# Attention steps of one unit laid between the projection chunks of the next, with their matmuls in a fixed order

## The chip, the cores and the metric
One NeuronCore of one Trainium2 chip runs the whole kernel. The metric is the device time of one execution in microseconds (us). TensorE is called PE in the rows (its weight loads PEld), VectorE DVE, ScalarE ACT, GpSimd POOL, SyncE SP.

## What is computed
One decoder layer over a prompt of 1024 tokens and, at once, one new token for each of 8 sequences with caches (T = 1032 columns). The part that the change touches is the first norm and the grouped, dilated attention of the prompt:

```
h = rms_norm(x) ; proj = h @ w_in            # f32, 1024 inputs
for g in 0..2:                               # windows 128, 512, 2048; dilations 1, 4, 16
    s = q_g k_g^T * Dh^-0.5 + bias_g         # 8 heads of 64, blocks of 128 queries,
    s = where(band mask, s, -inf)            #   keys of the own and the previous block
    o_g, lse_g = softmax(s) @ v_g, logsumexp(s)
a_out = sum_g softmax_g(lse_g) * o_g         # the groups are combined
```

Beside it stand the sample tokens' attention over the caches, the mLSTM with its gates, the gated merge, and a ConvFFN. All arithmetic has f32 inputs and outputs.

## The kernel before
**Projections.** f32 products are made of three products of high and low parts. A weight tile of 1024 x 128 arrives as `raw`; `split` (L175) casts it to `whi` on ScalarE (L176) and subtracts to get `wlo` on VectorE (L177). `mm` (L182) issues 24 matmuls into one PSUM bank (L189): 8 of whi with the activation's high part, 8 of whi with its low part, 8 of wlo with its high part. `proj_chunk` does that for one of three column chunks (352, 352, 328) and writes the bank out; `proj` does the three. There are 3 such banks (`pp`), 5 banks (`X`) for everything else, two buffers for whi and wlo and three for raw. A pool of 16 tiles of 128 x 1032 (`A`) holds what lives longer.

**The first norm.** Nine row tiles are loaded by SP, normalised in an order that is written out (every ScalarE and VectorE step of it is pinned by `in_order`), transposed on TensorE and split into `act_hi`, `act_lo` (L241, L247). The raw weights of the first q and k are loaded between them and split after tiles 1 and 2.

**Attention.** There are 12 units: pair of heads p = 0 to 3, and in it group g = 0 to 2; unit number 3p + g. A unit makes the projections q, k, v (nine chunks, written out to `qT`, `kT` by ScalarE, L338 and L340, to `vT` by VectorE, L342), transposes v and k back to rows (`ptr`, L365; copies `vn`, `kn`), sends these to the caches by POOL, loads two bias tiles `bt`, and then runs its attention in slots. In slot x stand: the scores of group x (`stage_s`: matmuls L429, on VectorE a reduction with bias and minimum into `sb` and `st`, L438, on ScalarE the exponential, L442), the product of group x-2 (`stage_v`: `po` L482, written out to `oT` by L494 or L498), and the transposes of group x-1 (`stage_t`: `pt` L455, copied to `pts` by either engine, L458). Groups 0 and 1 have 4 groups of two blocks and so 6 slots, group 2 has 2 groups of four blocks and 4 slots.

**Between the units** stand the combining of the pair before and the sample tokens' attention: `combine_a` and `sample_a` at the end of a pair; then `combine_b` and `sample_b` after unit (p,0) of the next, `combine_c` and `sample_c` after unit (p,1), `sample_d` after unit (p,2). `combine_c` issues three loads `fbc` on POOL, each 1024 factors of a head read 64 times from `f_d`, multiplies each `oT` by its `fbc` on VectorE (L555), and adds (L556, L557). `sample_b` loads the broadcast q rows `qb` by POOL and multiplies by cache keys (L577). The mLSTM gates' projection (`gates_proj`, evacuated to `gsb`) comes after unit 0, four gate projections (`gate_a`) after unit 11.

**The order.** Each engine runs its instructions in one fixed order, which the framework chooses when the kernel is built: each instruction goes out by its place in the program as soon as it is ready by the framework's own durations, so that work of two units may mix. `in_order` binds an instruction to stay behind the one written before it on its engine. In a stage, every matmul but the first is bound so (`chained`, L411 on).

Of the kernel before, what the change touches and what calls it, by code (L numbers as in the profile page):

```python
# [22 lines left out]
DIL = (1, 4, 16)  # L23
# [17 lines left out]
def kernel(  # L41
# [48 lines left out]
    def A(name, cols=T, dt=F32):  # L90
        return ap_.tile([128, cols], dt, tag="A", name=name)
# [15 lines left out]
    def dma_out(out, in_):  # L107
        nc.gpsimd.dma_start(out=out, in_=in_)  # L108
# [49 lines left out]
    def raw_w(src):  # L158

        k = src.shape[0] // 128  # L160
        m = src.shape[1]
        raw = wp.tile([128, 1024], F32, tag="raw", name="wraw", bufs=3)
        dma_w(raw[:, 0:k * m].rearrange("p (k c) -> p k c", c=m), src.rearrange("(k p) c -> p k c", p=128))
        return raw, k, m

    def split_w(raw, k, m, pin=False):

        hi = wp.tile([128, 1024], F32R, tag="hi", name="whi")
        lo = wp.tile([128, 1024], F32R, tag="lo", name="wlo")
        return split(raw, hi, lo, k * m, pin) + (m,)  # L170

    def load_w(src):
        return split_w(*raw_w(src))
# [147 lines left out]
    def perm(ap, g):  # L321
        return ap.rearrange("p (r u) -> p u r", r=DIL[g]) if g else ap

    def attn_unit(pair, g, st):
        d = DIL[g]
        U = S // d
        qT, kT, vT = A("qT"), A("kT"), A("vT")
        evacs = []
        for kind, dst in enumerate((qT, kT, vT)):
            def evac(ci, t0, n, ps, kind=kind, dst=dst):  # L330
                npm = min(n, S - t0)
                if g == 0:
                    dv, sv = dst[:, t0:t0 + npm], ps[:, 0:npm]
                else:
                    dv = dst[:, 0:S].rearrange("p (r u) -> p r u", r=d)[:, :, t0 // d:(t0 + npm) // d]
                    sv = ps[:, 0:npm].rearrange("p (u r) -> p r u", r=d)
                if kind == 0:
                    nc.scalar.mul(dv, sv, -0.125)  # L338
                elif kind == 1:
                    nc.scalar.copy(dv, sv)  # L340
                else:
                    nc.vector.tensor_copy(dv, sv)  # L342
                if npm < n:
                    if kind == 0:
                        nc.vector.tensor_scalar(out=smp[:, pair, kind, g, :], in0=ps[:, npm:n], scalar1=-0.125, scalar2=None, op0=ALU.mult)
                    else:
                        nc.vector.tensor_copy(smp[:, pair, kind, g, :], ps[:, npm:n])
            col = kind * AQ + g * 512 + pair * 128
            if pair == 0 and g == 0 and kind < 2:
                evacs.append(evac)  # L350
                if kind == 1:
                    for ci in range(len(CHUNKS)):
                        for k in range(2):
                            proj_chunk(first_w[k], hT, evacs[k], ci)
            else:
                proj(w_in2[:, col:col + 128], hT, evac)
        vn = A("vn")
        kn = A("kn")
        keep = ((7,), (1, 3, 5, 7), tuple(range(8)))[g]
# [27 lines left out]
        for hd in range(2):  # L387
# [10 lines left out]
        oT = A("oT")  # L398
        live = {}
        pos = [None, None]  # L400

# [99 lines left out]
        for x in range(n + 2):  # L501
# [271 lines left out]
    def gate(dst, col):  # L773
# [2 lines left out]

        proj(w_in2[:, col:col + 128], hT, evac)

    def gate_a(j):
# [37 lines left out]
    def row_tile():  # L817
        return wk.tile([128, 128], F32, tag="rowsT", name="rowsT", bufs=4)

    done = None  # L820
    for pair in range(4):
        st = wk.tile([128, 96], F32, tag="st", name="st", bufs=2)
        oT = []
        for g in range(3):
            oT.append(attn_unit(pair, g, st))
            if g == 0 and done:
                combine_b(done[0])
                sc = sample_b(done[0])
            if g == 1 and done:
                combine_c(*done)  # L830
                sb = sample_c(done[0], sc)
            if g == 2 and done:
                sample_d(done[0], *sb)
            stage = pair * 3 + g
            if stage == 0:
                gates_proj()
            elif stage == 1:
                gates_log()
            elif stage == 2:
                gates_max()  # L840
            elif stage == 3:
                gates_rows()
            elif stage == 5:
                gcol, decb, sc8, scb3 = gates_cols()
            elif stage == 7:
                mcv_r = rows_load([mconv_w[0].rearrange("i (j p) -> (i j) p", p=128), mconv_b.rearrange("o (j p) -> (o j) p", p=128)], row_tile)
                mst_r = rows_load([st_conv[0].rearrange("b i (j p) -> (b i j) p", p=128)], row_tile)
            elif stage == 8:
                mcv = rows_T(mcv_r, c2.tile([128, 80], F32, name="mcv"))
                mcv3 = mcv.rearrange("p (i j) -> p i j", j=16)  # L850
                nc.vector.tensor_scalar(out=mcv3[:, :, 0:8], in0=mcv3[:, :, 0:8], scalar1=0.5, scalar2=None, op0=ALU.mult)
                nc.vector.tensor_scalar(out=mcv3[:, :, 8:16], in0=mcv3[:, :, 8:16], scalar1=1.0 / 32.0, scalar2=None, op0=ALU.mult)
                mst = rows_T(mst_r, c2.tile([128, 384], F32, name="mst"))
                mst4 = mst.rearrange("p (b i j) -> p j b i", b=8, i=3)
        combine_a(pair, st)
        sample_a(pair)
        done = (pair, oT)
# [8 lines left out]
    combine_c(*done)  # L866
    for g in range(3):
        for kv in range(2):
            for pair in range(4):
# [616 lines left out]
```

## Time and profile before

| what | us |
|---|---|
| median of 3 runs | 2315.59 |
| lowest and highest of them | 2315.16, 2315.99 |
| the profiled execution | 2312.85 |
| its span | 2311.0 |
| TensorE busy in the span | 2264.6 |
| VectorE, ScalarE, POOL busy | 1152.1, 686.6, 211.4 |

The span runs from the first to the last instruction of the profiled execution; 1.85 us of its time lie around it. Rows are of that execution. The attention phase lies between about 42 and 700 us; what follows (mLSTM, merge, ConvFFN) is not touched. A group of rows gives the number of instructions in it; a bracket gives the idle time of the engine just before it and what ended it.

### The profile page before, as it was taken

What the parts mean: (1) busy time and instruction counts of PE and PEld (TensorE: products, weight loads), DVE (VectorE), ACT (ScalarE), POOL (GpSimd) and SP (SyncE); (2) the same over time, 40 slices, a digit from 0 to 9 for tenths busy, and PEclk for the clock granted to TensorE, in tenths of its full rate; (3) what the DMA queues carried; (4) which work ended last, traced back from release to release, by engine and by line L of the source; (5) the groups of instructions that cost most, each with busy time, mean ns of one, the idle gap of its engine ahead of it and who ended that gap; (6) DMA issues with size and microseconds to landing.
All of it is one profiled execution on the core that took longest, in us unless ns stands there. A gap on an engine that the chain in (4) does not pass through costs nothing.

```text
span 2311.0 us, 36395 instructions
## 1 busy us (share of the span) xinstructions
PE 2264.6 (98%) x15077; PEld 2174.5 (94%) x15077; DVE 1152.1 (50%) x2689; ACT 686.6 (30%) x1337; POOL 211.4 (9%) x380
## 2 busy tenths in 40 slices
PE   7999999999999999999999999999999999999998
PEld 6799899989989999999999999999999999999997
DVE  6253434434435454646331444346556556655666
ACT  4234333343312333323232311342222222221222
POOL 1111210111110011111122100000000000000000
PEclk9999999999999999999999999999999999999999
DMA  5323533434362142424244521221111111111112
GB/s 186 93 52 83 121 79 97 115 82 120 95 187 82 51 127 59 128 60 137 77 128 130 200 72 46 74 78 59 55 37 46 37 46 55 55 48 43 48 37 78
DMA packets 243014, 196.79 MB, mean 85 GB/s; under 512 B 24393, under 2 KB 220089, under 8 KB 242834
## 3 DMA queue, kind: packets, MB, share of 16 engines
q1 hardware_dynamic: 206577, 124.65, 19.2%
q0 software_dynamic: 36272, 69.84, 9.9%
q8 instruction: 118, 1.93, 0.4%
q14 instruction: 47, 0.38, 0.1%
HBM read 160.30 MB, written 39.20 MB: 86 GB/s over the span
## 4 chain that ended last, share of the span: by engine, by line
PE 84%; DMA 5%; issue 3%; ACT 2%; DVE 1%; POOL 1%; DVEq 0%; POOLq 0%; ACTq 0%
PE pp L189 64%; PE ppd L1379 10%; DMA fbc<-f_d 3%; PE pcm L996 1%; ACT sb L442 1%; PE ni L990 1%; PE po L482 1%; PE pt L455 1%; PE s L429 1%; PE na L993 1%; PE sm L977 1%; PE pxo L1247 1%; PE ptr L365 0%; POOL out_dram L108 0%; PE pkm L966 0%
## 5 line engine op out<-in xcount | busy, mean ns | idle before, releaser
L189 PE MATMUL pp<-act_hi,whi 128*128 128x352 f32 (+1 forms) x3272 | 598.5, 324 | 4.4 <-ACT qT L338 2.0
L189 PE MATMUL pp<-act_lo,whi 128*128 128x352 f32 (+1 forms) x3272 | 585.2, 320 | 0.0
L189 PE MATMUL pp<-act_hi,wlo 128*128 128x352 f32 (+1 forms) x3272 | 581.1, 319 | 1.1 <-DVE wlo L177 1.1
L189 PEld LDWEIGHTS pp<-act_hi,whi 128*128 128x128 f32 x3272 | 527.5, 188 | 14.2 <-issue 4.3
L189 PEld LDWEIGHTS pp<-act_hi,wlo 128*128 128x128 f32 x3272 | 524.2, 187 | 4.3 <-DVE wlo L177 1.4
L189 PEld LDWEIGHTS pp<-act_lo,whi 128*128 128x128 f32 x3272 | 525.8, 187 | 2.0 <-issue 0.2
L177 DVE TENSOR_TENSOR wlo<-wraw,whi 128x1024 fp32r<-128x1024 f32 (+2 forms) x153 | 181.9, 1189 | 438.9 <-PE pp L189 239.3
L176 ACT CAST whi<-wraw 128x1024 fp32r<-128x1024 f32 (+2 forms) x153 | 156.7, 1024 | 674.8 <-PE pp L189 622.1
L1380 DVE TENSOR_TENSOR x<-x,ppd 128x352 f32<-128x352 f32 (+4 forms) x248 | 124.7, 515 | 72.7 <-PE ppd L1379 72.6
L1305 DVE TENSOR_TENSOR fu<-pp,sq 128x320 f32<-128x320 f32 (+1 forms) x130 | 64.6, 510 | 182.3 <-PE pp L189 182.0
L1379 PE MATMUL ppd<-fhi,dhi 128*128 128x352 f32 (+3 forms) x528 | 123.8, 320 | 0.2
L1379 PE MATMUL ppd<-fhi,dlo 128*128 128x352 f32 (+3 forms) x528 | 123.9, 320 | 0.0
L1379 PE MATMUL ppd<-flo,dhi 128*128 128x352 f32 (+3 forms) x528 | 123.3, 319 | 0.0
L1319 DVE SCALAR_TENSOR_TENSOR y<-fu,fcv,y 128x1048 f32<-128x1048 f32 x88 | 115.0, 1307 | 2.4 <-ACT y L1317 1.2
L442 ACT ACTIVATE sb<-sb,st 128x128 f32<-128x128 f32 (+1 forms) x192 | 84.0, 440 | 31.2 <-DVE st L438 31.2
L1379 PEld LDWEIGHTS ppd<-fhi,dhi 128*128 128x128 f32 x528 | 89.5, 188 | 1.8 <-issue 0.5
L1379 PEld LDWEIGHTS ppd<-fhi,dlo 128*128 128x128 f32 x528 | 89.5, 188 | 1.4
L1379 PEld LDWEIGHTS ppd<-flo,dhi 128*128 128x128 f32 x528 | 89.4, 188 | 1.4
L105 POOL DMA_DIRECT2D gfin<-in_final_norm_g_dram x1 | 0.5, 527 | 912.7 <-DVE fu L1305 912.7
L342 DVE COPY vT<-pp 128x352 f32<-128x352 f32 (+1 forms) x36 | 18.5, 514 | 104.6 <-PE pp L189 104.6
L1317 ACT ACTIVATE y<-fu,fcv 128x1048 f32<-128x1048 f32 x44 | 55.7, 1266 | 30.3 <-DVE fu L1307 30.0
L438 DVE CUSTOM_DVE_ANT_0 sb<-s,bt 128x128 f32<-128x128 f32 (+1 forms) x192 | 54.8, 347 | 17.4 <-PE pt L455 8.7
(380 smaller groups left out, 2309.2 us busy)
## 6 DMA issues: line engine op xcount, KB each, us to landing
wraw<-in_w_in_dram SPq DMA_DIRECT2D x84, 512.0 KB
wraw<-in_w_up_dram SPq DMA_DIRECT2D x44, 512.0 KB
draw<-in_w_down_dram SPq DMA_DIRECT2D x22, 512.0 KB
c<-in_state_mlstm_C_dram SPq DMA_DIRECT2D x32, 256.0 KB
out_dram<-c POOLq DMA_DIRECT2D x32, 256.0 KB, 3.6
kt<-in_cache_kv_w_dram SPq DMA_DIRECT2D x12, 512.0 KB
qb<-sn_d POOLq DMA_DIRECT2D x12, 512.0 KB, 5.5
vt<-in_cache_kv_w_dram SPq DMA_DIRECT2D x12, 512.0 KB
```

The lines of the kernel that those rows point to most:

```text
L176: a = nc.scalar.copy(hi[:, 0:n], raw[:, 0:n])
L177: b = nc.vector.tensor_tensor(out=lo[:, 0:n], in0=raw[:, 0:n], in1=hi[:, 0:n].bitcast(F32), op=ALU.subtract)
L189: nc.tensor.matmul(ps[0:m, 0:n], wt[:, i * m:(i + 1) * m], act[i][which][:, t0:t0 + n], start=(pi == 0 and i == 0), stop=(pi == 2 and i == ...
L429: yield nc.tensor.matmul(ss_[hd][:, at[b]:at[b] + kw], qT[pr, b * 128:(b + 1) * 128], kT[pr, k0 * 128:k0 * 128 + kw], start=True, stop=True)
L438: nc.vector.tensor_tensor_reduce(out=sb[:, 0:kw], in0=ss_[hd][:, at[b]:at[b] + kw], in1=bias[hd][:, 256 - kw:256], scale=1.0, scalar=3e38, ...
L442: nc.scalar.activation(out=sb[:, 0:kw], in_=sb[:, 0:kw], func=ACTF.Exp, scale=-1.0, bias=st[:, cm:cm + 1], accum_out=st[:, cl:cl + 1])
L455: yield nc.tensor.transpose(pt[:, x * 128:(x + 1) * 128], live[(b, hd)][:, i * 128:(i + 1) * 128], ident)
L1305: nc.vector.tensor_tensor(out=u[:, 2 + t0:2 + t0 + npm], in0=ps[:, 0:npm], in1=r2[:, t0:t0 + npm], op=ALU.mult)
L1317: nc.scalar.activation(out=y, in_=u[:, 0:YW], func=ACTF.Identity, scale=fcv3[:, 0, j:j + 1], bias=fcv3[:, 3, j:j + 1])
L1319: nc.vector.scalar_tensor_tensor(out=y, in0=u[:, i:i + YW], scalar=fcv3[:, i, j:j + 1], in1=y, op0=ALU.mult, op1=ALU.add)
L1379: nc.tensor.matmul(ps[:, 0:n], wds[j][w][:, m * 128:(m + 1) * 128], parts[j][a][:, t0:t0 + n], start=(x == 0), stop=(x == len(seq) - 1))
L1380: nc.vector.tensor_tensor(out=x1[m][:, t0:t0 + n], in0=x1[m][:, t0:t0 + n], in1=ps[:, 0:n], op=ALU.add)
```

## The change
`attn_unit` is cut into a class: `steps()` yields after each of a unit's nine projection chunks and then makes its tiles (`attn_tiles`: transposes, cache outputs, bias loads); `attn_slots` yields after each attention slot. `weave` lays the slots of unit n before chosen chunks of unit n+1: six slots before chunks 0, 2, 3, 5, 6, 8, four before 0, 3, 5, 7. Unit 11 is woven with the six chunks of the first two gate projections (slots before 0, 2, 3, 5). All matmuls of a stage are bound by `in_order`, the first too. What stood between the units (`extras`) now comes when the weave of unit n is through, so behind the projections and tiles of unit n+1 and ahead of that unit's slots. `gates_proj` stands between the projections of unit 0 and its slots. At the end `combine_b(3)` and `sample_b(3)` come before the third gate projection, `sample_c(3)` between the last two.

At the start the raw weight of the first v is loaded as well, behind that of k, and is split, bound, after norm tile 3, into two tiles of the pool `A`; unit 0 projects q, k, v of chunk 0, then of chunk 1, then of chunk 2, where it was q, k of each chunk and then v.

```diff
     def split_w(raw, k, m, pin=False):
-        hi = wp.tile([128, 1024], F32R, tag="hi", name="whi")
-        lo = wp.tile([128, 1024], F32R, tag="lo", name="wlo")
+        if pin and pin == "A":
+            hi, lo = A("whi", 1024, F32R), A("wlo", 1024, F32R)
+        else:
+            hi = wp.tile([128, 1024], F32R, tag="hi", name="whi")
+            lo = wp.tile([128, 1024], F32R, tag="lo", name="wlo")
...
     raws.append(raw_w(w_in2[:, AQ:AQ + 128]))
+    raws.append(raw_w(w_in2[:, 2 * AQ:2 * AQ + 128]))
     for i in range(5, 9):
         load_x(i)
...
-        if i in (1, 2):
-            first_w.append(split_w(*raws[len(first_w)], pin=True))
+        if i in (1, 2, 3):
+            first_w.append(split_w(*raws[len(first_w)], pin="A" if i == 3 else True))
...
+            if pair == 0 and g == 0:
+                for ci in range(len(CHUNKS)):
+                    for k in range(3):
+                        proj_chunk(first_w[k], hT, evacs[k], ci)
+                        yield
+            else:
+                for kind, evac in enumerate(evacs):
+                    col = kind * AQ + g * 512 + pair * 128
+                    w = load_w(w_in2[:, col:col + 128])
+                    for ci in range(len(CHUNKS)):
+                        proj_chunk(w, hT, evac, ci)
+                        yield
+            attn_tiles(self)
...
         def chained(ms):
-            for i, m in enumerate(ms):
-                if i:
-                    in_order(m)
+            for m in ms:
+                in_order(m)
...
                 stage_t(groups[x - 1])
-        return oT
+            yield
...
+    def weave(slots, steps, n):
+        slots = list_of(slots)
+        for i in range(n):
+            while slots.todo and slots.at * n <= i * slots.n:
+                slots.run()
+            next(steps, None)
+        while slots.todo:
+            slots.run()
+        for _ in steps:
+            pass
...
+    for _ in units[0].steps():
+        pass
+    gates_proj()
+    for stage in range(12):
+        pair, g = divmod(stage, 3)
+        un = units[stage]
+        if stage < 11:
+            weave(un, units[stage + 1].steps(), 9)
+        else:
+            weave(un, gate_steps(tga_d, CGA, range(2)), 6)
+        if g == 2:
+            got["oT"][pair] = [units[pair * 3 + i].oT for i in range(3)]
+            combine_a(pair, un.st)
+            sample_a(pair)
+        extras(stage)
...
-    gate_a(0)
     combine_b(3)
     sc = sample_b(3)
-    gate_a(1)
+    gate_a(2)
     sb = sample_c(3, sc)
-    gate_a(2)
+    gate_a(3)
     sample_d(3, *sb)
-    gate_a(3)
-    combine_c(*done)
+    combine_c(3, got["oT"][3])
```

## Rows read from the trace of the kernel before

**Rows 1.** The page's list of engines: busy time, share of the span, instructions.
```profile
PE 2264.6 (98%) x15077; PEld 2174.5 (94%) x15077; DVE 1152.1 (50%) x2689; ACT 686.6 (30%) x1337; POOL 211.4 (9%) x380
```

**Rows 2.** The view of the waits of TensorE over the whole span. Columns: engine, line and tile that waited <- engine and tile (with line) waited for: us in total, times, longest us.
```profile
PE pt L455 <- ACT sb L442: 10.4, 12, 3.5
...
PE psc L598 <- DVE sc L578: 3.1, 2, 2.5
PE pp L189 <- ACT qT L338: 2.0, 2, 1.4
...
PE po L482 <- ACT pts L458: 1.0, 3, 0.3
...
PE pp L189 <- DVE gsb L657: 0.7, 1, 0.7
```

**Rows 3.** The table by stage: stretch, its length, busy time of PE, PEld, DVE, ACT, POOL (with instructions), mean granted TensorE clock as a share of full speed, DMA share, GB/s.
```profile
81.00:100.00 19.00, 14.80 (x118) 11.38 (x118) 11.78 (x42) 10.89 (x38) 3.65 (x8) 0.82 0.17 38
100.00:620.00 520.00, 509.77 (x3806) 476.78 (x3806) 217.68 (x723) 184.20 (x534) 84.13 (x142) 1.00 0.36 94
...
648.00:655.00 7.00, 7.00 (x30) 6.93 (x30) 2.34 (x8) 0.93 (x3) 0.00 (x0) 0.60 0.60 176
```

**Rows 4.** The waits of TensorE again, from 100 to 620 us alone.
```profile
PE pt L455 <- ACT sb L442: 6.9, 11, 0.8
```

**Rows 5.** TensorE's timeline in unit 0 (66 to 100 us). Columns: start us, us, engine, line, operation, tiles, shape, number of instructions in the group, and in brackets the idle time before it and what ended it. Consecutive groups overlap a little; their pace is read from the starts.
```profile
84.60 1.54 PE L455 MATMUL pt<-ident,sb 128*128 128x128 f32 x6 [3.48 <-ACT sb L442]
86.07 2.08 PE L429 MATMUL s<-kT,qT 64*128 64x256 f32 x8
88.08 1.55 PE L482 MATMUL po<-pts,vn 128*64 128x128 f32 x12
...
90.96 1.13 PE L429 MATMUL s<-kT,qT 64*128 64x256 f32 x8
```

**Rows 6.** VectorE's timeline in unit 0 (78 to 92 us), columns as above.
```profile
81.22 1.23 DVE L177 TENSOR_TENSOR wlo<-wraw,whi 128x1024 fp32r<-128x1024 f32 x1 [11.31 <-ACT whi L176]
```

**Rows 7.** TensorE's timeline at the start of unit 5's first projection (296 to 304 us).
```profile
296.73 1.55 PE L189 MATMUL pp<-act_hi,whi 128*128 128x352 f32 x8 [1.41 <-ACT qT L338]
298.12 1.44 PE L189 MATMUL pp<-act_lo,whi 128*128 128x352 f32 x8
299.40 1.44 PE L189 MATMUL pp<-act_hi,wlo 128*128 128x352 f32 x8
```

**Rows 8.** VectorE's timeline in the first norm (12 to 45 us).
```profile
19.41 1.28 DVE L229 SCALAR_TENSOR_TENSOR xn<-xn,rst,gbc 128x1024 f32<-128x1024 f32 x1
...
24.20 1.28 DVE L229 SCALAR_TENSOR_TENSOR xn<-xn,rst,gbc 128x1024 f32<-128x1024 f32 x1
...
27.85 1.28 DVE L229 SCALAR_TENSOR_TENSOR xn<-xn,rst,gbc 128x1024 f32<-128x1024 f32 x1
```

**Rows 9.** TensorE's timeline in unit 4 (267 to 300 us), its first slots.
```profile
271.40 1.92 PE L429 MATMUL s<-kT,qT 64*128 64x128 f32 x16
275.10 0.88 PE L455 MATMUL pt<-ident,sb 128*128 128x128 f32 x6 [0.31 <-ACT sb L442]
...
276.76 0.88 PE L482 MATMUL po<-pts,vn 128*64 128x128 f32 x12
```

**Rows 10.** The view of the tile `fbc`: its issuing instruction, and its DMAs' time from issue to landing.
```profile
L105 POOL DMA_DIRECT2D fbc<-f_d x12: 811/895/917, 273.9 to 669.4; - x12
...
DMA to landing us min/median/max: 17.6/19.9/21.7
```

**Rows 11.** The same view of the tile `qb`.
```profile
DMA to landing us min/median/max: 4.0/5.5/9.2
```

**Rows 12.** POOL's timeline, in unit 4 (first row) and in unit 5.
```profile
273.86 2.51 POOL L105 DMA_DIRECT2D fbc<-f_d  x3
...
322.89 0.67 POOL L108 DMA_DIRECT2D out_dram<-vn  x1 [21.00 <-DVE vn L373]
...
324.83 0.76 POOL L108 DMA_DIRECT2D out_dram<-vn  x1
```

**Rows 13.** VectorE's timeline in unit 4, from the last copy of scores to the first multiplication by `fbc` and the next operation.
```profile
280.56 1.08 DVE L458 COPY pts<-pt 128x256 f32<-128x256 f32 x2
293.89 1.23 DVE L555 TENSOR_TENSOR oT<-oT,fbc 128x1024 f32<-128x1024 f32 x1 [12.26 <-DMA fbc<-f_d]
295.04 0.54 DVE L601 CUSTOM_DVE_ANT_0 ssb<-psc,ssb 16x387 f32<-16x387 f32 x1
```

**Rows 14.** TensorE's timeline in unit 4: the last input of that L601.
```profile
285.88 0.20 PE L599 MATMUL psc<-ones,qk 128*16 128x1 f32 x2
```

**Rows 15.** TensorE's timeline in unit 5: the scores of its first two slots in one group.
```profile
322.03 2.08 PE L429 MATMUL s<-kT,qT 64*128 64x128 f32 x32
```

**Rows 16.** TensorE's timeline near the end of the phase (606 to 660 us).
```profile
627.25 0.28 PE L562 MATMUL psn<-ident,smp 128*72 128x128 f32 x1
...
647.74 0.38 PE L598 MATMUL psc<-ident,sc 128*16 128x128 f32 x1 [2.54 <-DVE sc L578]
...
648.20 2.71 PE L189 MATMUL pp<-act_hi,whi 128*128 128x352 f32 x8
...
654.58 1.45 PE L189 MATMUL pp<-act_hi,whi 128*128 128x352 f32 x8
655.87 1.44 PE L189 MATMUL pp<-act_lo,whi 128*128 128x352 f32 x8
```

More of the change, by code (lines that the diff above doesn't have):

```diff
@@ L322, in perm, with __init__, steps, evac @@
         return ap.rearrange("p (r u) -> p u r", r=DIL[g]) if g else ap
[L324 to L343, printed above, removed]
+    class Unit:
+        def __init__(self, pair, g, st):
+            self.pair, self.g, self.st = pair, g, st
+        def steps(self):
+            pair, g = self.pair, self.g
+            d = DIL[g]
+            self.qkv = [A("qT"), A("kT"), A("vT")]
+            evacs = []
+            for kind, dst in enumerate(self.qkv):
+                def evac(ci, t0, n, ps, kind=kind, dst=dst):
+                    npm = min(n, S - t0)
+                    if g == 0:
+                        dv, sv = dst[:, t0:t0 + npm], ps[:, 0:npm]
+                    else:
+                        dv = dst[:, 0:S].rearrange("p (r u) -> p r u", r=d)[:, :, t0 // d:(t0 + npm) // d]
+                        sv = ps[:, 0:npm].rearrange("p (u r) -> p r u", r=d)
@@ L344, in evac @@
                     if kind == 0:
-                        nc.vector.tensor_scalar(out=smp[:, pair, kind, g, :], in0=ps[:, npm:n], scalar1=-0.125, scalar2=None, op0=ALU.mult)
-                    else:
-                        nc.vector.tensor_copy(smp[:, pair, kind, g, :], ps[:, npm:n])
-            col = kind * AQ + g * 512 + pair * 128
-            if pair == 0 and g == 0 and kind < 2:
-                evacs.append(evac)
-                if kind == 1:
-                    for ci in range(len(CHUNKS)):
[L353 to L356, printed above, removed]
+                        nc.scalar.mul(dv, sv, -0.125)
+                    elif kind == 1:
+                        nc.scalar.copy(dv, sv)
+                    else:
+                        nc.vector.tensor_copy(dv, sv)
@@ L357, in attn_unit, with slots, attn_tiles @@
+            attn_tiles(self)
+        def slots(self):
+            return attn_slots(self)
+    def attn_tiles(un):
+        pair, g = un.pair, un.g
+        qT, kT, vT = un.qkv
         vn = A("vn")
@@ L397, in attn_unit, with attn_slots @@
             bias.append(bt)
-        oT = A("oT")
+        un.vn, un.bias = vn, bias
+    def attn_slots(un):
+        pair, g, st = un.pair, un.g, un.st
+        d = DIL[g]
+        (qT, kT, _), vn, bias = un.qkv, un.vn, un.bias
+        oT = un.oT = A("oT")
         live = {}
@@ L777, in gate, with gate_steps, evac @@
         proj(w_in2[:, col:col + 128], hT, evac)
+    def gate_steps(dst_d, col0, js):
+        for j in js:
+            tg = A("tga")
+            def evac(ci, t0, n, ps, tg=tg):
+                nc.scalar.activation(out=tg[:, t0:t0 + n], in_=ps[:, 0:n], func=ACTF.Tanh, scale=0.5)
+            w = load_w(w_in2[:, col0 + j * 128:col0 + (j + 1) * 128])
+            for ci in range(len(CHUNKS)):
+                proj_chunk(w, hT, evac, ci)
+                yield
+            dma_out(dst_d[j * 128:(j + 1) * 128, :], tg[:, 0:T])
     def gate_a(j):
@@ L818, in row_tile @@
         return wk.tile([128, 128], F32, tag="rowsT", name="rowsT", bufs=4)
[L820 to L829, printed above, removed]
-                combine_c(*done)
[L831 to L857, printed above, removed]
@@ L858, with __init__, todo, run @@
-    gate_a(0)
+    def weave(slots, steps, n):
[8 more added lines that the diff above has]
+            pass
+    class list_of:
+        def __init__(self, unit):
+            self.n = 4 if unit.g == 2 else 6
+            self.at = 0
+            self.gen = unit.slots()
+        @property
+        def todo(self):
+            return self.at < self.n
+        def run(self):
+            next(self.gen, None)
+            self.at += 1
@@ new lines, in extras @@
+    def extras(stage):
+        pair, g = divmod(stage, 3)
+        if pair:
+            if g == 0:
+                combine_b(pair - 1)
+                got["sc"] = sample_b(pair - 1)
+            elif g == 1:
+                combine_c(pair - 1, got["oT"][pair - 1])
+                got["sb"] = sample_c(pair - 1, got["sc"])
+            else:
+                sample_d(pair - 1, *got["sb"])
+        if stage == 1:
+            gates_log()
+        elif stage == 2:
+            gates_max()
+        elif stage == 3:
+            gates_rows()
+        elif stage == 5:
+            got["gates"] = gates_cols()
+        elif stage == 7:
+            got["mcv_r"] = rows_load([mconv_w[0].rearrange("i (j p) -> (i j) p", p=128), mconv_b.rearrange("o (j p) -> (o j) p", p=128)], row_tile)
+            got["mst_r"] = rows_load([st_conv[0].rearrange("b i (j p) -> (b i j) p", p=128)], row_tile)
+        elif stage == 8:
+            mcv = got["mcv"] = rows_T(got["mcv_r"], c2.tile([128, 80], F32, name="mcv"))
+            m3 = mcv.rearrange("p (i j) -> p i j", j=16)
+            nc.vector.tensor_scalar(out=m3[:, :, 0:8], in0=m3[:, :, 0:8], scalar1=0.5, scalar2=None, op0=ALU.mult)
+            nc.vector.tensor_scalar(out=m3[:, :, 8:16], in0=m3[:, :, 8:16], scalar1=1.0 / 32.0, scalar2=None, op0=ALU.mult)
+            got["mst"] = rows_T(got["mst_r"], c2.tile([128, 384], F32, name="mst"))
@@ new lines @@
+    got = {"oT": {}}
+    sts = [wk.tile([128, 96], F32, tag="st", name="st", bufs=2) for _ in range(2)]
+    units = []
+    for stage in range(12):
+        pair, g = divmod(stage, 3)
+        if g == 0:
+            st = sts[pair] if pair < 2 else wk.tile([128, 96], F32, tag="st", name="st", bufs=2)
+        units.append(Unit(pair, g, st))
+    for _ in units[0].steps():
+        pass
+    gates_proj()
+    for stage in range(12):
+        pair, g = divmod(stage, 3)
+        un = units[stage]
+        if stage < 11:
+            weave(un, units[stage + 1].steps(), 9)
+        else:
+            weave(un, gate_steps(tga_d, CGA, range(2)), 6)
[4 more added lines that the diff above has]
+        extras(stage)
```

9 lines of the change are left out of this document (8 added, 1 removed).

## The prediction

> **What bounds the kernel now.** I read the page's engine list first: TensorE is busy for 2264.6 of 2311.0 us, 98% [rows 1], so all engines together leave some 46 us that an edit could win, and only idle time of TensorE or a lower clock of it counts. Next came TensorE's waits, over the whole span [rows 2]. The reader is to see how small they are and that one of them is the attention's own: the transposes of the scores (`pt`) wait for exponentials (`sb`) for 10.4 us in 12 places, 3.5 of them in one. A projection waits 2.0 us for `qT` to be written out, the `po` matmuls 1.0, one projection 0.7 for `gsb`. Third, a table by stage [rows 3]: from 100 to 620 us, the attention phase proper, TensorE is busy for 509.77 of 520 us at full clock, and of that stage's idle time 6.9 us are the `pt` wait [rows 4]. From 81 to 100 us it is busy for 14.80 of 19 and the mean clock is 0.82, from 648 to 655 it is 0.60. So the attention waits cost little each, and one near the start is dear because the clock falls with it. No other engine is near a bound here: VectorE is busy 217.68 of the 520 us, ScalarE 184.20.
>
> **What the change takes away.** In unit 0 the gates' projection stands between the first scores and their transposes, and still the transposes wait 3.48 us [rows 5]: on VectorE a weight split (1.23 us at 81.22) is in the queue before the score reductions [rows 6]. Behind that idle time the same groups are slower than a little later: 6 transposes 1.54 instead of 0.88 us [rows 5, 9], 8 wide score matmuls 2.08 instead of 1.13 [rows 5], 12 `po` matmuls 1.55 instead of 0.88 [rows 5, 9]: 0.66 + 0.95 + 0.67 = 2.3 us of clock. In the changed kernel the gates' projection comes first and the first scores have two chunks of unit 1 behind them. A chunk is 3 x 1.28 = 3.84 us (starts of its groups of 8) [rows 7], a 328-column one, by its columns, about 3.6. Everywhere else, too, at least one chunk lies between scores and transposes. What must fit under it is about 3.7 us, from the first score matmul to its transposes in unit 4 (271.40 to 275.10) [rows 9]; between two slots there are 3.6 to 3.84 us of chunk plus the slot's own 12 `po`, 6 transposes and the next scores (some 0.8 to 0.9 each) [rows 9]: 6 to 7 us. That covers one more split (1.2) and some copies. If that cover fails, the waits are what they are now, 0.8 us at most outside unit 0 [rows 4]. So I take all of it: 10.4 + 2.3 + 2.0 + 1.0 + 0.7 = 16.4 us. The bounds are 16.4 and the 3.5 + 2.3 + 0.7 = 6.5 of unit 0 alone.
>
> **What it adds at the start.** VectorE paces the norm: with a pinned split 4.79 us from tile to tile (19.41 to 24.20), without 3.65 (24.20 to 27.85) [rows 8]. The third split lengthens one tile by 1.1. Three chunks run before the norm's end, as before (three banks), now q, k, v of chunk 0 instead of q, k and q. The third raw weight goes into SP's queue ahead of x5 to x8; their loads are covered, as the norm waits for no load in this stretch and the gap is filled by the split. ScalarE's third cast stands in front of later squares, within the same 1.1. I take +1.2, bounds -4 (one chunk more ready at the end of the norm) and +3 (cast and loads late as well).
>
> **What it moves: the broadcast.** `combine_c` keeps its place in the program, after unit (p,1), p = 1 to 3, but the attention of unit (p,2) is now spread over 34 us behind it. It issues three `fbc` transfers on POOL and pins a multiplication on VectorE for each. One transfer takes 17.6 to 21.7 us, median 19.9 [rows 10]; `qb`, as large, takes 5.5 [rows 11]. In unit 4 the first issue is at 273.86 [rows 12] and the first multiplication runs at 293.89 after 12.26 us of waiting [rows 13]; TensorE loses only 1.41 us by it [rows 7], since the bunch of attention is over by then. In the change, score reductions, `pt` copies, splits and `vT` copies of (p,2) queue behind that multiplication. How early does it stand in VectorE's queue? By unit 4 it is behind a copy that ran at 280.56 and ahead of a reduction (L601) [rows 13] whose input was there at about 286.1 [rows 14]: 6.7 to 12.2 us after the issue. What is ready earlier than that is ahead of it, what is ready later waits.
>
> The rest is a count from the end of the transposes `ptr` (zero). The unit's output DMAs stand in front on POOL; by unit 5 that takes from 322.03 [rows 15] to 325.6 [rows 12], and with two `bt` issues fbc goes out at 3.6 to 4.7, lands at 23.5 to 26.4, and its multiplication (1.23 us [rows 13]) ends at 24.7 to 27.6. Scores of one slot take 1.04 us (half of 2.08 [rows 15]). Slot 1 comes three chunks on, at 1.04 + 11.28 = 12.3; its reductions are ready at 12.6, 8 to 9 us after the issue, its transposes' copies at 14.4, 10 to 11 after. Both lie between 6.7 and 12.2, so the row decides neither way. Slot 2 comes two chunks later, at 22.1, and needs those copies. If these stand behind, they end 0.7 later than the multiplication, at 25.4 to 28.3, and TensorE waits 3.3 to 6.2; if the reductions stand behind too, up to 7, and up to 9 with the other two multiplications in front. I take half of the middle, 2.4 us each for p = 1 and 2; bounds 0 and 9. For p = 3 the weave is with six gate chunks: slot 1 at 8.7 (ahead), slot 2 at 14.5, its copies at 16.7, 12 to 13 after the issue and so behind, slot 3 at 24.4, which then waits 1.0 to 3.9: I take 2.4; bounds 0 and 14, the latter if the copies of slot 1 are behind as well. Sum 7.2, bounds 0 and 32.
>
> A wait of 2.54 us was followed by 24 matmuls that took from 648.20 to 654.58, 6.38 instead of 3.84 us [rows 16, 7], so 2.5 lost at the lower clock (0.60 in that stretch [rows 3]); one of 1.41 had no such train [rows 7]. Of three possible waits I count one as long enough: +2.5, bounds 0 and 7.5.
>
> Were these 20 us the price of other traffic, `fbc` could land as `qb` does in the quieter, spread units, at about 10, before the copies of slot 1 are due; that is rival B. The Trainium skill ("DMA: Bandwidth & Descriptors", Rules for kernel authors) says that a DMA whose outermost dimension has c < 16 entries is confined to at most c engines. The source of `fbc` begins with a dimension of 2, that of `qb` with 128, and the durations agree (19.9 against 5.5 us), though no row here counts engines. By this rule the 20 us stay wherever the transfer lies, the sum stands at 2312.1, and B needs its other way, by the copies; without the rule B would be as likely as A.
>
> **The end of the phase.** Now 15.6 us of gate chunks stand between `psn` (627.25) and `psc`, and `psc` still waits 3.1 us [rows 2, 16] for `sc`. After the change the program has one gate (11.28) and the sample work of pair 2 (about 3 us of TensorE) there: 1.3 us less. The chain through `sn_d` and `qb` starts at `psn` either way. I take +2.0, bounds 0 and 4.3 (if the sample work lies ahead of `psn`). The other moved steps (combine_a, sample_a, gates_log and so on) issue the same instructions between the same units; `sg` and `qb` wait at most 9 us of landing, less than two chunks, and stand behind slot 0: I cost them at nothing.
>
> **The sum.** 2312.85 - 16.4 + 1.2 + 7.2 + 2.5 + 2.0 = 2309.35 for an execution like the profiled one. The median of the runs is 2.74 above that execution, so 2312.1: 0.15% less. Under 0.2%, 4.6 us, a measurement of this kernel cannot tell from no change.
>
> **The rivals.** B, the broadcast is hidden: all copies of (p,2) stand ahead of the multiplication or go to ScalarE, and the end stays as it is. For it: ScalarE has time (184.20 of 520 us busy [rows 3]) and copies of this kind have no fixed engine. Then 2312.85 - 16.4 + 1.2 + 2.74 = 2300.4, 2296 to 2303.
> C, the broadcast becomes the bound, and the kernel is slower: the multiplication stands ahead of slot 1's reductions in all three pairs, so VectorE is deaf for some 10 us, with slots 2 and 3 due in that time. It decides from a place in the queue earlier than 8 us after the issue. Price: waits of 7, 7 and 10.9, three falls of the clock 7.5, against 9.7 in my sum: 2312.1 + 22.7 = 2334.8, down to 2321 with one of the three.
> D, the change does not do what it says: pinned matmuls only swap places, the waits of 100 to 620 us come back at other slots, and only unit 0 is won: 2312.1 + 16.4 - 6.5 = 2322, or, with the broadcast hidden and the end unchanged, 2310.3. Against it: 6 to 7 us of cover for a 3.7 us chain.
> E, TensorE has more room than its idle time. The rows show groups of 8 matmuls at 1.28 to 1.29 us in both stretches of projections [rows 7, 16], so the room is the idle time. Were the 520 - 476.78 = 43.2 us without a weight load to be had in place of the idle 10.2 [rows 3], 33 us more would go: 2279. The Trainium skill ("Perfetto Trace Analysis", Identifying the Most-Contended Engine) would judge headroom so, by weight-load busy time, not matmul busy time; the even pace [rows 7, 16] speaks against it here.
>
> **How the numbers follow.** A (the sum, 2304 to 2320) 0.48, B 0.22, C 0.17, D 0.11, E 0.02. The predicted time is A's, 2312. Range: B's floor of 2296 to 2331, most of C, which leaves out E and the upper end of C. Faster than 2311: 0.20 of A, B, E = 0.44. Within 0.2%: 0.23 of A, 0.07 of D = 0.30. Slower: 0.05 of A, C, 0.04 of D = 0.26.
>
> **What would show it.** In the changed trace: no idle time of 3.48 us and no slow transposes near 81 us (clock near 1.00 there); `pt` waits for `sb` under 2 us in all; the first fbc multiplication of each pair behind or ahead of the copies of slot 1, and with it `pt` or `po` waits for VectorE in units 5, 8 and 11, of 3 us or none; the norm's end about 1.1 us later; a `psc` wait of 3 to 7 us. I am wrong if slots wait for VectorE where no broadcast is near (the cover is too short), or if TensorE's pace of 1.28 us changes.

## The result, and the profile after

The changed kernel takes 2347.11 us (median of 4 runs, 2344.73 to 2349.0) against 2315.38 in the same runs: a ratio of 1.0137, 95% interval 1.012 to 1.0155. It is 32 us slower; the forecast was 2312.1, with a range up to 2331. The profiled execution took 2348.28 us, its span 2345.1, that is 34.1 more than before.

```profile
PE 2275.5 (97%) x15077; PEld 2181.1 (93%) x15077; DVE 1148.5 (49%) x2685; ACT 690.9 (29%) x1341; POOL 211.3 (9%) x380
```

This line of the page answers to [rows 1]: TensorE is busy 10.9 us longer for the same 15077 matmuls, so part of the loss is clock, and idle for 69.6 us in place of 46.4, so 23.2 are waits. Which waits, the view of TensorE's waits over the whole span says (columns as in [rows 2]):

```profile
PE po L511 <- DVE pts L487: 13.4, 2, 8.0
PE pt L484 <- ACT sb L471: 11.5, 4, 3.5
...
PE po L511 <- ACT pts L487: 9.2, 1, 9.2
...
PE psc L626 <- DVE sc L606: 5.0, 3, 2.0
```

Of the waits that the change was forecast to remove, the eleven small ones of `pt` [rows 4], those for `qT` and the 1.0 of `po` are gone; the 0.7 for `gsb` is now 0.6 for `vT`, in unit 0 as well. The 11.5 us of `pt` are four new places, and two lines of `po`, 22.6 us in three places, were not there at all. TensorE's timeline gives the places, in order of time units 0, 4, 5, 7, 8, 10 and 11 (`pt` in 0, 4, 7, 10, `po` in 5, 8, 11; columns as in [rows 5]):

```profile
122.36 1.54 PE L484 MATMUL pt<-ident,sb 128*128 128x128 f32 x6 [3.48 <-ACT sb L471]
...
290.38 0.87 PE L484 MATMUL pt<-ident,sb 128*128 128x128 f32 x6 [2.93 <-ACT sb L471]
...
351.37 1.97 PE L511 MATMUL po<-pts,vn 128*64 128x128 f32 x16 [5.38 <-DVE pts L487]
...
438.12 0.92 PE L484 MATMUL pt<-ident,sb 128*128 128x128 f32 x6 [1.84 <-ACT sb L471]
...
506.39 1.98 PE L511 MATMUL po<-pts,vn 128*64 128x128 f32 x16 [8.05 <-DVE pts L487]
...
594.13 0.87 PE L484 MATMUL pt<-ident,sb 128*128 128x128 f32 x6 [3.27 <-ACT sb L471]
...
654.33 1.98 PE L511 MATMUL po<-pts,vn 128*64 128x128 f32 x16 [9.15 <-ACT pts L487]
```

The long ones first. Unit 5 on VectorE:

```profile
326.54 1.20 DVE L583 TENSOR_TENSOR oT<-oT,fbc 128x1024 f32<-128x1024 f32 x1
327.68 0.27 DVE L467 CUSTOM_DVE_ANT_0 sb<-s,bt 128x128 f32<-128x128 f32 x1
...
344.14 1.23 DVE L583 TENSOR_TENSOR oT<-oT,fbc 128x1024 f32<-128x1024 f32 x1 [14.50 <-DMA fbc<-f_d]
...
348.94 0.28 DVE L467 CUSTOM_DVE_ANT_0 sb<-s,bt 128x128 f32<-128x128 f32 x1
...
350.63 0.69 DVE L487 COPY pts<-pt 128x512 f32<-128x512 f32 x1
```

The first multiplication waits for nothing; the second stands ahead of all reductions of slot 1 (from 348.94) and is idle for 14.50 us until its `fbc` is there. POOL's timeline says why the two differ:

```profile
305.05 0.92 POOL L105 DMA_DIRECT2D fbc<-f_d  x1
323.59 1.34 POOL L108 DMA_DIRECT2D out_dram<-kn  x2 [17.62 <-ACT kn L398]
324.87 1.41 POOL L108 DMA_DIRECT2D out_dram<-vn  x2
326.13 1.75 POOL L105 DMA_DIRECT2D fbc<-f_d  x2
```

The first load goes out 18 us ahead of the unit's cache outputs, the other two stand behind them in POOL's queue and land 18 us after their issue. In the kernel before, all three went out together ([rows 12], x3). The scores of slot 1 were done at 337.2, so everything that VectorE had to do for them waited 11.7 us.

Units 4, 7 and 10 wait in another place, which I had costed at nothing. VectorE in unit 4, from the first key product of the sample tokens (multiplication L605, reduction L606) to the last of the four score reductions of slot 0 (L467):

```profile
277.00 1.21 DVE L605 TENSOR_TENSOR qb<-qb,kt 128x1024 f32<-128x1024 f32 x1
278.13 0.28 DVE L467 CUSTOM_DVE_ANT_0 sb<-s,bt 128x128 f32<-128x128 f32 x1
278.35 1.21 DVE L606 TENSOR_REDUCE sc<-qb 128x16 f32<-128x1024 f32 x1
...
282.42 1.23 DVE L605 TENSOR_TENSOR qb<-qb,kt 128x1024 f32<-128x1024 f32 x1 [2.73 <-DMA f_d<-fr]
283.56 0.28 DVE L467 CUSTOM_DVE_ANT_0 sb<-s,bt 128x128 f32<-128x128 f32 x1
283.77 1.22 DVE L606 TENSOR_REDUCE sc<-qb 128x16 f32<-128x1024 f32 x1
284.90 1.21 DVE L605 TENSOR_TENSOR qb<-qb,kt 128x1024 f32<-128x1024 f32 x1
...
286.38 1.22 DVE L606 TENSOR_REDUCE sc<-qb 128x16 f32<-128x1024 f32 x1
...
287.70 0.41 DVE L467 CUSTOM_DVE_ANT_0 sb<-s,bt 128x256 f32<-128x256 f32 x1
```

In the kernel before the four reductions of the slot follow each other (unit 4):

```profile
272.86 0.28 DVE L438 CUSTOM_DVE_ANT_0 sb<-s,bt 128x128 f32<-128x128 f32 x1
...
273.62 0.42 DVE L438 CUSTOM_DVE_ANT_0 sb<-s,bt 128x256 f32<-128x256 f32 x1
```

Here they are spread from 278.13 to 288.1 between six operations of 1.2 us, and the transposes start at 290.38. VectorE also stands idle among them, for 2.73 us, ahead of the second product. In units 7 and 10 the same wait is put down to the landing of `qb`:

```profile
433.25 1.23 DVE L605 TENSOR_TENSOR qb<-qb,kt 128x1024 f32<-128x1024 f32 x1 [1.57 <-DMA qb<-sn_d]
...
589.27 1.23 DVE L605 TENSOR_TENSOR qb<-qb,kt 128x1024 f32<-128x1024 f32 x1 [3.01 <-DMA qb<-sn_d]
```

TensorE's waits in these units, 2.93, 1.84 and 3.27 us, are each 0.20 to 0.27 longer than VectorE's, 2.73, 1.57 and 3.01. The traces of e1, e2, e3 and e9 have 12 more such pairs, with idle times of VectorE from 1.55 to 3.19 us, and there TensorE's wait is 0.19 to 0.28 longer. So VectorE's wait is passed on in full: the six operations and the reductions between them have used up the two chunks that should cover the chain.

In unit 0 the wait is 3.48 us as before [rows 5], 122 us after the start in place of 85: all nine chunks of unit 1 run ahead of the transposes. VectorE's queue there:

```profile
96.41 1.23 DVE L180 TENSOR_TENSOR wlo<-wraw,whi 128x1024 fp32r<-128x1024 f32 x1 [11.97 <-ACT whi L179]
...
107.70 1.23 DVE L180 TENSOR_TENSOR wlo<-wraw,whi 128x1024 fp32r<-128x1024 f32 x1 [9.99 <-ACT whi L179]
...
118.97 1.22 DVE L180 TENSOR_TENSOR wlo<-wraw,whi 128x1024 fp32r<-128x1024 f32 x1 [9.97 <-ACT whi L179]
120.12 0.28 DVE L467 CUSTOM_DVE_ANT_0 sb<-s,bt 128x128 f32<-128x128 f32 x1
```

These three weight splits stand ahead of the reductions, whose scores were done at 83.6. At the start the norm ends 1.1 us later (41.26 against 40.15), and the clock is lower behind it: in the table by stage 0.70 from 40 to 56 us, against 0.89 before. `ptr` of unit 0 comes at 70.19, before at 66.75.

### The profile page after: what moved, and what is told of

It reads as the page before. It is cut to its first block, busy times and chain, and to the rows that moved or that the text cites. A ratio compares the mean times of both kernels' runs of the same rounds, so it can differ in the third digit from the quotient of the medians.

```text
span 2345.1 us, 36423 instructions
## 1 busy us (share of the span) xinstructions
PE 2275.5 (97%) x15077; PEld 2181.1 (93%) x15077; DVE 1148.5 (49%) x2685; ACT 690.9 (29%) x1341; POOL 211.3 (9%) x380
## 4 chain that ended last, share of the span: by engine, by line
PE 65%; issue 2%; DMA 2%; DVE 1%; ACT 1%; POOL 0%; DVEq 0%; POOLq 0%; ACTq 0%
PE pp L192 48%; PE ppd L1462 10%; PE pcm L1079 1%; PE ni L1073 1%; DMA braw<-bT_d 1%; PE na L1076 1%; PE sm L1060 1%; PE pxo L1330 1%; PE pkm L1049 0%; DMA araw<-aT_d 0%; PE pn L1183 0%; DMA qb<-sn_d 0%; PE ppx L192 0%; PE pkm L1051 0%; PE ph L1103 0%
## 5 line engine op out<-in xcount | busy, mean ns | idle before, releaser
L192 PE MATMUL pp<-act_hi,whi 128*128 128x352 f32 (+1 forms) x3272 | 605.1, 326 | 2.1 <-ACT act_hi L244 1.1
L192 PEld LDWEIGHTS pp<-act_hi,whi 128*128 128x128 f32 x3272 | 527.7, 189 | 14.7 <-issue 7.9
L179 ACT CAST whi<-wraw 128x1024 fp32r<-128x1024 f32 (+2 forms) x153 | 156.6, 1024 | 594.7 <-PE pp L192 532.6
L467 DVE CUSTOM_DVE_ANT_0 sb<-s,bt 128x128 f32<-128x128 f32 (+1 forms) x192 | 56.8, 344 | 83.8 <-PE s L458 83.7
## 6 DMA issues: line engine op xcount, KB each, us to landing
fbc<-f_d POOLq DMA_DIRECT2D x12, 512.0 KB, 17.6
```

What stands on the lines that cost most here:

```text
L179: a = nc.scalar.copy(hi[:, 0:n], raw[:, 0:n])
L192: nc.tensor.matmul(ps[0:m, 0:n], wt[:, i * m:(i + 1) * m], act[i][which][:, t0:t0 + n], start=(pi == 0 and i == 0), stop=(pi == 2 and i == ...
L467: nc.vector.tensor_tensor_reduce(out=sb[:, 0:kw], in0=ss_[hd][:, at[b]:at[b] + kw], in1=bias[hd][:, 256 - kw:256], scale=1.0, scalar=3e38, ...
```

## The experiments

All ratios are to the kernel before, run beside each on the same chip.

**e1_halves: the landing.** In the changed kernel, `combine_c`:

```diff
-            dma_in(t[:, 0:S], _bcast(f_d[pair][:, :], g * 2048, [[1024, 2], [0, 64], [1, 1024]]))
+            for hd in range(2):
+                dma_in(t[hd * 64:(hd + 1) * 64, 0:S], _bcast(f_d[pair][:, :], g * 2048 + hd * 1024, [[0, 64], [1, 1024]]))
```

> The changed kernel, with each fbc load issued as two loads of 64 partitions, whose outermost dimension is 64 instead of 2. Theory W (TensorE waits because VectorE stands at the second fbc multiplication until a transfer of about 18 us lands): the landing falls to some 5 us, the three waits of 5.4, 8.1 and 9.2 us in units 5, 8 and 11 go, and with them about 7 us at the low clock: 2347.1 - 22.6 - 7 = 2317, between 2314 and 2325. Rival Q (it is the work, five operations of 1.2 us at that place of VectorE's queue, not the landing): waits of 2 to 5 us stay in each unit, 2330 to 2340. Rival L (the landing is long by other traffic): the halves land no faster, 2345.

2317.25 us, ratio 1.0011 (1.0002 to 1.0021): 29.9 less than the changed kernel, as theory W had it. The view of the tile `fbc`:

```profile
DMA to landing us min/median/max: 5.0/8.2/11.1
```

8.2 us in place of 17.6, and 0.6 us of `po` wait in place of 22.6. Rival L falls with the landing, Q with the wait. In this trace the first multiplication of unit 5, too, runs only at 335.48, in place of 326.54. So the built order of VectorE moved as well, and this run alone doesn't part landing from place in the queue.

**e2_combine_on_gpsimd: another engine waits.** The same three multiplications and two additions as `nc.gpsimd.tensor_tensor`, without the pin.

> The changed kernel, with the three multiplications by fbc and the two additions behind them on GpSimd, so that VectorE stands in no queue behind a landing; the transfers keep their shape and time. Theory W: the three waits go as with the halved loads, 2317, between 2312 and 2328 (GpSimd's own loads of bias and its outputs come some 20 us later, which no unit needs so early). Rival L or Q do not differ from W here; rival N (the three waits have another cause, such as the exponentials or the output copies of po): 2347.

2332.12 us, ratio 1.0072 (1.0057 to 1.0087). The three `po` waits are gone with transfers as long as ever (16.7 us), so the wait sat in VectorE's queue, and N falls. But only half of the 30 us was won. POOL now stands at the landing itself (14.28 us in the last pair) and takes twice as long for a multiplication; behind these operations stand the small transfers that `combine_b` needs, and `pst` on TensorE waits for 12 us (two lines, of the tile `fbc` and of TensorE's timeline). In unit 5 a projection waits 3.7 us for `qT`, which was not followed up.

```profile
L583 POOL TENSOR_TENSOR oT<-oT,fbc x12: 2384/2401/3368, 328.5 to 703.7; 128x1024 f32<-128x1024 f32 x12
...
670.21 0.38 PE L573 MATMUL pst<-ident,ff 128*48 128x128 f32 x1 [11.97 <-DVE ff L571]
```

**e9_multiply_late: the place alone.** The loads stay as they were; `combine_c` puts the five operations into `fill[at]`, and `weave` writes them behind chunk `at`. The cut leaves out `combine_c` itself.

```diff
             next(steps, None)
+            if i in fill:
+                fill.pop(i)()
...
-                combine_c(pair - 1, got["oT"][pair - 1])
+                combine_c(pair - 1, got["oT"][pair - 1], at=6 if stage < 10 else 5)
```

> The changed kernel; fbc is loaded where and as it was (one load with 2 outermost, some 18 us), but the three multiplications and two additions are written behind chunk 6 of the following weave (behind chunk 5 of the last, shorter one). In the built order they stand behind the second slot's reductions and copies in units 5 and 8; in unit 11 one copy still stands behind the second of them. Theory W (what matters is that VectorE's queue holds work behind a wait for a landing, not the landing itself): the waits of 5.4 and 8.1 us and their clock go, and about half of the 9.2: 2347.1 - 18 - 6 = 2323, between 2318 and 2328. Rival (the long transfer itself delays other transfers, or these five operations delay any slot): 2335 to 2347.

2328.53 us, ratio 1.0056 (1.004 to 1.0073), 18.6 less than the changed kernel and just outside my span. Units 5 and 8 wait no more, with a landing of 18.2 us. Unit 11 waits longer, not half:

```profile
634.67 1.23 DVE L590 TENSOR_TENSOR oT<-oT,fbc 128x1024 f32<-128x1024 f32 x1 [16.06 <-DMA fbc<-f_d]
635.81 0.28 DVE L469 CUSTOM_DVE_ANT_0 sb<-s,bt 128x128 f32<-128x128 f32 x1
...
637.50 0.69 DVE L489 COPY pts<-pt 128x512 f32<-128x512 f32 x1
...
639.24 1.22 DVE L591 TENSOR_TENSOR oT<-oT 128x1024 f32<-128x1024 f32 x1
```

There one multiplication (idle for 16.06 us before it) still stands ahead of the reductions of slot 1 (from 635.81), and `po` waits 10.97. So transfers of the same kind (14.8 to 20.9 us) cost TensorE 0 or 11 us in one execution, by whether the reductions stand behind the waiting multiplication in VectorE's queue. The weave of unit 11 has six chunks in place of nine, so the place is not quite all that differs.

**e3_bias_broadcast: unit 0.** In the changed kernel, where the bias rows are written out:

```diff
-            dma_out(rep_d[r][:, :, :], _bcast(vec_d[:, :], h0 * 384, [[384, n], [0, 128], [1, 384]]))
+            dma_out(rep_d[r].rearrange("n p c -> p n c"), _bcast(vec_d[:, :], h0 * 384, [[0, 128], [384, n], [1, 384]]))
```

> The changed kernel, with the broadcast of the bias rows into rep_d written with its 128-fold dimension outermost (on both sides), and so a shorter load as the framework counts it; in the built order the reductions of unit 0's first scores then stand behind the first weight split after the gates, not behind the third. Theory B0 (unit 0 gains nothing in the changed kernel because these reductions stand late in VectorE's queue, as its transposes do on TensorE): the wait of 3.5 us near 122 us goes, and the slow stretch behind it, 2.7 us, and the 0.7 of vT: 2347.1 - 6.8 = 2340, between 2337 and 2343. Rival (the wait is a chain of exponentials that any place has): 2347.

2339.28 us, ratio 1.0102 (1.0087 to 1.0117): 7.8 less, theory B0. No wait stands in unit 0's timeline any more. In the changed kernel POOL had issued `bt` of unit 0's first slot at 73.07 us, and the four loads up to 85.2 landed within 4.5 us each; the reductions ran at 120.12. So it was not the load but the order, made when the kernel is built, that had them late.

**e4_no_qb_product and e5_products_spread: the sample tokens' products.** First left out (e4), then moved (e5): the loads where they were, products 0, 1, 2 written behind chunks 1, 4 and 7 by the same `fill`.

> The changed kernel with the sample tokens' key product left out: the loads of qb and kt stay, and in place of the product over 1024 columns and its reduction, VectorE does one product over 16 columns, unpinned. Theory S (the waits of 2.9, 1.8 and 3.3 us in units 4, 7 and 10, and part of the 5.0 us of psc, come from six operations of 1.2 us that stand between the score reductions): these go but for some landing at the end, 8 + 3 + about 3 of clock: 2333, between 2330 and 2338. Rival (VectorE stands at the landing of qb, not at the work): the waits stay, 2343 to 2347.

> The changed kernel; the loads of qb and kt are issued where they were, but the three key products of a pair (multiplication and reduction, VectorE) are written behind chunks 1, 4 and 7 of the following weave instead of all three ahead of its first slot. The work is the same. Theory S (it is the place of the six operations, between the first score reductions of units 4, 7 and 10): the waits of 2.9, 1.8 and 3.3 us go, with 1 to 3 us of clock: 2347.1 - 10 = 2337, between 2334 and 2341; psc at the end keeps its 5 us. Rival (it is the amount of VectorE's work, which any place has): 2344 to 2348.

e4: 2327.93 us, ratio 1.0052 (1.0037 to 1.0067). e5: 2332.95 us, ratio 1.0078 (1.0063 to 1.0094), 14.2 less than the changed kernel with all the work kept. In both, the `pt` waits of units 4, 7 and 10 are gone:

```profile
PE pt L484 <- ACT sb L471: 3.5, 1, 3.5
```

That 3.5 is unit 0's alone. Both runs are below the spans I had given. The place is shown by them: the products cost TensorE these waits only where they stand among slot 0's reductions. That it was the work and not the landing, as theory S has it, is not shown: in e4's built order all four reductions of slot 0 run ahead of the second product (in unit 4 until 278.84 us), which then still waits for its landing (2.83 us), and TensorE loses nothing; in e5 it is the same (1.98 us). The pairs of waits in the section above say that the landing is what TensorE felt, with the work having used up the cover; a run that takes away the landing alone is missing. Of the 14.7 us between the two spans (2345.1 and 2330.4), 8.0 are the `pt` waits, 2.9 are shorter `po` waits (19.7 in place of 22.6), and 2.3 less busy time (2273.2 in place of 2275.5), so clock.

**e6_before_third_weight: the start.** The kernel before with the third early weight, so that unit 0 projects q, k, v chunk by chunk, and nothing else.

> The kernel before, with only the third early weight added (loaded ahead of x5, split after norm tile 3, q, k, v projected chunk by chunk). Theory P (this part alone costs what unit 0's transposes ptr show, 70.19 against 66.75 us: the norm's end 1.1 us later, and a longer stretch at the low clock behind it): 2315.4 + 3.4 = 2318.8, between 2317 and 2320. Rival (the start is longer by what the change does after it, the gates first): 2315 to 2316.5; my sum had 1.2.

2316.21 us, ratio 1.0006 (0.9997 to 1.0016): 1.2 more at the median, not 3.4, and in the rival's span; the interval takes in no change. In its trace the norm's end (41.74) and `ptr` (71.52) are late as in the changed kernel, but the 1.41 us wait for `qT` [rows 7] is 0.18, and unit 0's slow transposes take 1.15 in place of 1.54 us. Theory P read one part of a trace as the whole.

**e7_before_both_loads: the mended loads in the old order.** The two edits of e1 and e3 in the kernel before.

> The kernel before, with no part of the change, but with fbc as two loads of 64 partitions and the bias rows broadcast with the 128-fold dimension outermost. In its built order the reductions of unit 0's first scores stand behind one weight split, not two. Theory W and B0 together: in this order the broadcast only costs the 1.4 us wait for qT, the late reductions the 3.5 + 0.7 + 2.3 us of unit 0: 2315.4 - 7.9 = 2307.5, between 2305 and 2310. If the loads' shape mattered by itself, as traffic, it would gain here as much as in the changed kernel, 30 us; if these waits of unit 0 are a chain that any order has, 2314.

2303.99 us, ratio 0.9954 (0.9937 to 0.9971): 11 less than before, beyond my span. The waits of unit 0, for `gsb` and for `qT`, are gone, as expected, and also 1.1 of `wlo`. The two edits together are worth 11 us here and 37.7 (29.9 + 7.8) in the changed kernel: it is the weave that makes the landing dear.

**e8, e10, e11: everything mended.** e8 is the changed kernel with e1, e3 and e5, `sample_a` of a pair written ahead of the weave of its last unit, and two early weights; e10 the same with three; e11 is e8 with the late multiplications of e9.

> The changed kernel with everything found so far mended: fbc as two loads, bias rows broadcast with 128 outermost, key products spread, sample_a of a pair written ahead of the weave of its last unit (its sn_d row is then earlier), and the third early weight taken back. If the terms add: 2347.1 - 29 (broadcast) - 6.8 (unit 0; 7.8 were measured) - 10 (products) - 3.4 (start) - 2 (end) = 2296, between 2292 and 2301, which is below both kernels. If the waits only take each other's place (rival D of the prediction), 2305 to 2316.

> The kernel with everything mended, but with the third early weight as the change has it. By the norm's rows (one split of 1.1 us on VectorE, the norm's end 1.2 us later) 2294.3 + 1.2 = 2295.5, between 2294.5 and 2297. By unit 0's transposes ptr of the changed kernel (3.4 us later than before) 2297.7. If the chunks of v in place of q relieve the banks, below 2294.

> The kernel with everything mended and the multiplications by fbc late as well. The one wait left in the mended kernel's attention, 2.1 us of po for a copy in unit 11, would go if the copy stood ahead of all three multiplications; in the built order it stands ahead of two: 2293, between 2291 and 2296, hardly to be told from 2294.3.

e8: 2294.25 us, ratio 0.9908 (0.9893 to 0.9923). e10: 2296.49, ratio 0.9919 (0.9904 to 0.9934). e11: 2291.6, ratio 0.9896 (0.9882 to 0.9911), the lowest median, though its interval overlaps e8's: 23 us under the kernel before and 12 under e7. The terms add: 29.9 + 7.8 + 14.2 = 51.9 from the changed kernel gives 2295.2, and e8 is 2294.25 with two small edits more. That they meet within 1 us is in part luck: 2.9 of e5's 14.2 are `po` waits that e1 takes away too, and e8 has also lost the 5.0 us of `psc`, which is in none of the three terms. Whether e10's 2.2 us over e8 are the third weight is open: the runs of the two overlap (2294.21 to 2299.35, 2291.46 to 2296.12).

The table by stage of e11 (columns as in [rows 3]) shows what the weave is worth once nothing stands in its way:

```profile
100.00:620.00 520.00, 519.19 (x3900) 483.15 (x3899) 220.26 (x734) 190.36 (x548) 92.96 (x162) 1.00 0.35 93
```

0.8 us idle of 520, where 10.2 were [rows 3]; `psc`, too, waits no more.

## Why the prediction was wrong

**The bound, and what could be won.** Right. TensorE's idle time was the room: e11 ends with 0.8 us of it in the attention phase. Groups of 8 matmuls still take 1.28 us, and no run won any of rival E's 33 us: in e11 weight loads are busy for 483.15 of the 520 us with TensorE busy for 519.19. The Trainium skill ("Perfetto Trace Analysis", Identifying the Most-Contended Engine) judges TensorE's headroom by the busy share of the weight loads; by this row that leaves, as an estimate, some 37 us, which no run here could win.

**The gain of 16.4 us.** Half right. The small waits went (6.9 + 2.0 + 1.0). The 6.5 us of unit 0 did not: the step "the first scores have two chunks of unit 1 behind them" took the program's order for the engine's. TensorE ran nine chunks there, because the order, once built, had the reductions behind three splits. I had seen one split ahead of them [rows 6] and counted on the two chunks to cover it. e3 shows what put the others there: the order is built with a long bias broadcast, and with another form of that transfer the wait goes.

**The start, +1.2.** e6 has 1.2 for this part alone, but its interval takes in nothing as well; the changed kernel's own rows show 3.4 at `ptr` (70.19 against 66.75). That the number fits is in part luck.

**The broadcast, 7.2 + 2.5.** The mechanism was the right one, its size the main error: 22.6 us of waits and 7.1 of slow groups behind them in the timeline (e1 gives 29.9 for both). The step that failed is the place in the queue: "Both lie between 6.7 and 12.2, so the row decides neither way", and half of the middle. The scores of slot 1 were done 11.1, 11.1 and 7.5 us behind the issue of the second load, and their reductions stood behind its multiplication in all three pairs, so the place was earlier than the row of unit 4 before had shown. That was rival C, given 0.17, and its price (24.9 of waits, 7.5 of clock) was near. I also missed that the three loads don't go out together: the first is early and costs nothing, the other two queue behind the cache outputs. In e1, loads whose outermost dimension is 64 landed in 8.2 us at the median, not 17.6. That agrees with the rule of the Trainium skill ("DMA: Bandwidth & Descriptors", Rules for kernel authors) that an outermost dimension of c < 16 confines a DMA to at most c engines. Each of these loads also carries half the bytes, so e1 doesn't part form from size; but `qb`, with all 512 KB and 128 outermost, landed in 6.2 us at the median in the changed kernel. No run counted engines.

**The other moved steps, nothing.** Wrong. `sample_b` cost 8.0 us of waits, 14.2 in all by e5. The step that failed is that `qb` and `sg` "stand behind slot 0": in unit 4 the first product stands ahead of all four of slot 0's reductions, the second ahead of three of them. The landing took 7.4 us there (275.00 to 282.42), within the 9 allowed, but the operations of 1.2 us had used up the two chunks, and TensorE waited as long as VectorE did for `qb` and 0.2 to 0.3 us more. It is the broadcast's mechanism once more, and slots that wait for VectorE with no broadcast near were a sign of being wrong that the prediction had named.

**The end, +2.0.** Right: `psc` waits 5.0, which was 3.1.

**The clock.** The prediction took a wait of 2.54 us as long enough for a slow train of matmuls and one of 1.41 as too short. The long waits had such trains, 2.0 to 2.6 us each; in between, the length did not decide. In the table by stage of the changed kernel, the stretch with unit 4's wait of 2.93 us and the one with unit 7's of 1.84:

```profile
288.00:296.00 8.00, 5.62 (x48) 4.96 (x49) 6.08 (x27) 6.26 (x24) 1.59 (x3) 1.00 0.43 18
...
436.00:444.00 8.00, 6.16 (x41) 5.05 (x41) 5.85 (x18) 4.11 (x13) 0.00 (x0) 0.79 0.01 2
```

The longer wait left the mean clock at 1.00, the shorter one has 0.79; in e3 one of 3.39 us in unit 4 was followed by transposes that took 1.54 us in place of 0.87.

Together, for the profiled execution: 6.5 (unit 0) + 20.0 (29.7 of waits and clock for the broadcast by the timeline, less my 9.7) + 9.2 (products: 8.0, and 1.2 of clock in unit 7) + 2.2 (the start) = 37.9 of the 38.9 us between 2309.35 and 2348.28.

Rival D fell: the waits did not swap places, they had causes of their own, each mended by itself (e1, e3, e5). The added pins do nothing: with the first matmul of each stage bound or left free, the built order of every engine is the same, in both kernels.

## What to carry to other kernels

When steps that came in a bunch are spread out, list what else stands in the queues of the engines that serve them: anything that waits for a landing, and any run of long operations that uses up its cover, now lies between a step and its next. Read the place in the queue from the built order, not from the program. Then move the waiting operation behind the steps, or shorten what it waits for, and cut runs of long operations into pieces.

## What was not expected of the hardware

A 128 x 1024 f32 multiplication takes 2.40 us on GpSimd and 1.22 on VectorE (e2 and the changed kernel). Two loads of 256 KB with 64 outermost land in 8.2 us at the median where one of 512 KB with 2 outermost takes 17.6. In the changed kernel, waits of 2.93 and 3.27 us inside dense matmul work left the mean granted clock of their 8 us at 1.00, one of 1.84 did not (0.79).
